# Every second column block of an up projection by seven block products, in a fused decoder layer

## The chip, the cores and the metric

The kernel runs on one core of a Trainium2 chip. The metric is the device time of one execution in microseconds (us); lower is better. All data is float32. The engines are named as in the profile: PE is TensorE's matmul, PEld its weight load, DVE is VectorE, ACT is ScalarE, POOL is GpSimd, SP is SyncE, which here only issues DMA transfers.

## The reference

One decoder layer over 512 positions and 1024 channels: a mixer (mLSTM heads and a gated long convolution), and then a feed-forward part with a causal convolution over 3 positions. The change lies in the feed-forward part:

```python
D_MODEL = 1024; SEQ = 512
D_FF = 2816                                  # 22 column blocks of 128
...
u = rms_norm(x, ffn_pre_g[l]) * (1.0 + sc2) + sh2
up = causal_dwconv(u @ ffn_up[l], ffn_conv_w[l], ffn_conv_b[l])   # (512,1024) @ (1024,5632)
a, gt = jnp.split(up, 2, axis=-1)
f = (jax.nn.silu(gt) * a) @ ffn_down[l]                           # (512,2816) @ (2816,1024)
x = x + g2 * rms_norm(f, ffn_post_g[l])
```

## The kernel before, in words

**Precision.** Each float32 operand of a large product is split into a high part (a rounded copy by ACT) and a low part (the rest, a subtraction by DVE or POOL). A product is then three matmuls, high by high, high by low and low by high (`mm3`, L188 to L190).

**Up projection.** It goes in 22 units, `for i in range(NF)`. Unit i takes column block i of the `a` half and column block i of the gate half: a weight tile `wup` of 128 x 2048, which is 16 blocks of 128 x 128 (8 along the 1024 channels for each half), 1 MB. `w_load` brings it in with one transfer on SP's queue into one of two `raws` buffers, and `w_split` cuts it into four quarters: ACT writes the high part (L170), POOL the low one (L171), into the 20 tiles of `wpool` (a quarter takes two). The matmuls write two PSUM banks, `pa` and `pg` (features by tokens, 128 x 512), 8 x 3 matmuls of 512 columns each, so 48 in a unit. The moving operand is the normalized activation, `u2h` and `u2l`, stored as two token halves of 256 (`th`), each with 8 channel blocks. Units 0 to 2 (`NE = 3`) are worked early, in token halves, so with matmuls of 256 columns; units 3 to 21 follow one after the other.

**What follows a unit.** `conv3` (L995 on ACT, L997 twice on DVE) reads each bank into an SBUF tile, ACT applies SiLU to the gate (L1057), and DVE multiplies into `F` (L1060). Two units fill one `F`; after each odd unit `forms(m, F)` makes group m's operands of the down projection: four sums on DVE (L1021 to L1024), two splits (L1013, L1014) into four slots `fh`, `fl`, and two transfers that send other parts out to `g2_d`. A slot is a 128 x 512 tile, and there are 44. The eleven groups' pairs need all 44 by the end.

**Down projection.** It is already done by seven block products. A first pass over the 11 groups (`prod1`: p1, p5, p7, p6, 24 matmuls of 512 columns for each group) needs `forms1(m)`: the weights of `load1(m)` (768 KB), three sums and four splits on DVE and ACT (L1099 to L1101, L1013, L1014). The p5 banks are the two `cv` banks, p1 the two `at` banks, p6 and p7 the four `mm` banks. A second pass (`prod2`) takes the remaining products with operands loaded again. Groups 0 to 10 come in order, and a bank is summed over all of them.

**Order.** SP's and PE's instructions are issued in the order of the program text. DVE, ACT and POOL are ordered by a planner that lists the work with a cost model, in the order of the text where several things are ready; a tile of a pool is given to the first instruction that writes it, once one is free. All transfers of weights are on SP's queue, so a transfer that waits for its buffer holds back those behind it. `load1(0)` and `load1(1)` go to `raws`, `load1(2)` to a tile that lies where `u2h` was.

Of the kernel before, what the change touches and what calls it, by code (L numbers as in the profile page):

```python
# [52 lines left out]
def decoder_layer(ctx, tc, w_glu0, x, xT, c, adaT, vecs, w_glu, w_qko, w_v0, w_v, w_out, w_up, w_down, out):  # L53
# [105 lines left out]
    def ada_done(a, b):  # L159
        V.tensor_tensor(out=mod[:, a:b], in0=mod[:, a:b], in1=vcols("ada_b", a, b - a), op=ALU.add)  # L160
# [3 lines left out]
    def w_split(src, name, pool=None, tag="w", eng=None):  # L164

        n = src.shape[1]
        pool = pool or wpool
        hi = pool.tile([P, T], F32R, tag=tag, name=f"{name}h")
        lo = pool.tile([P, T], F32R, tag=tag, name=f"{name}l")
        S.activation(hi[:, :n], src, AF.Copy)  # L170
        (eng or G).tensor_tensor(out=lo[:, :n], in0=src, in1=hi[:, :n].bitcast(F32), op=ALU.subtract)  # L171
        return hi, lo

    def w_load(view, name, pool=None, tag="w"):

        n = view.shape[1]
        r = raws.tile([P, 2048], F32, tag="raw", name=name)
        nc.sync.dma_start(r[:, :n], view)
        return [w_split(r[:, a : min(a + T, n)], f"{name}_{a}", pool, tag) for a in range(0, n, T)]

    def blk(pieces, b):
        hi, lo = pieces[b // 4]
        a = (b % 4) * P
        return hi[:, a : a + P], lo[:, a : a + P]

    def mm3(ps, a, b, start, stop):

        PE.matmul(ps, a[0], b[0], start=start, stop=False)  # L188
        PE.matmul(ps, a[0], b[1], start=False, stop=False)  # L189
        PE.matmul(ps, a[1], b[0], start=False, stop=stop)  # L190
# [459 lines left out]
    def send_rows(a, n, queue=nc.scalar):  # L650

        ps = mmbank(f"gT{a}") if a == KT else atbank(f"gT{a}")
        PE.transpose(ps[:n, :P], gains[:, a : a + n], ident)
        t = slot(f"gTs{a}")[:, :P]
        V.tensor_copy(t[:n, :], ps[:n, :P])
        for i in range(n // KT):
            queue.dma_start(rows_d[a // KT + i].rearrange("(j p) -> j p", p=P), t[i * KT : (i + 1) * KT, :])

    def row(i, make, name, queue=nc.scalar):

        rows = make(name) if make is not cvtile else [make(f"{name}r{hf}") for hf in range(2)]
# [327 lines left out]
    def halves(z):  # L989
        return z.rearrange("p (h t) -> p h t", h=2)  # L990
# [21 lines left out]
    def split(src, hi, lo):  # L1012
        S.activation(hi, src, AF.Copy)  # L1013
        behind_turn(V.tensor_tensor(out=lo, in0=src, in1=hi.bitcast(F32), op=ALU.subtract))  # L1014

    def forms(m, F):

        a11, a21, a12, a22 = (F[:, b * HT : (b + 1) * HT] for b in range(4))
        s1, s2 = ysum[:, :HT], ysum[:, HT:]
        s4 = ysq[:, (m % 2) * HT : (m % 2 + 1) * HT]  # L1020
        V.tensor_tensor(out=s1, in0=a21, in1=a22, op=ALU.add)  # L1021
        V.tensor_tensor(out=a21, in0=a11, in1=a21, op=ALU.subtract)
        V.tensor_tensor(out=s2, in0=s1, in1=a11, op=ALU.subtract)
        V.tensor_tensor(out=s4, in0=a12, in1=s2, op=ALU.subtract)  # L1024
        own = []
        for n, z in enumerate((F[:, :T], ysum)):
            hi, lo = slot(f"fh{m}_{n}", F32R), slot(f"fl{m}_{n}", F32R)
            split(z, hi, lo)
            own.append((hi, lo))
        pairs.append(own)  # L1030
        nc.scalar.dma_start(g2_d[m][:, :T], F[:, T : 2 * T])
        nc.scalar.dma_start(g2_d[m][:, T:], s4)

    for i in range(NF):
        if i < NE:
            pa, pg = early[i]
        else:
            pieces = w_load(w_up[i], f"wup{i}")
            if i in (4, 8, 12, 16):
                ada_block(38 + i // 2, last_lo[0])  # L1040
                ada_block(39 + i // 2, last_lo[0])
            if i == 19:
                ada_done(40, 48)
                gain(3, 40, "ffn_post_g")
                send_rows(3 * KT, KT)
                wide = adas.tile([P, D], F32, tag="ada", name="g2r")
                g2r = row(3, lambda n: [wide[:, :T], wide[:, T:]], "g2")
            both = []
            for half in range(2):
                ps = mmbank(f"up{i}_{half}")  # L1050
                for k in range(KT):
                    mm3(halves(ps), blk(pieces, half * KT + k), (u2h[:, :, k, :], u2l[:, :, k, :]), k == 0, k == KT - 1)
                both.append(ps)
            pa, pg = both
        a = conv3(pa, i, f"fa{i}")
        g = conv3(pg, NF + i, f"fg{i}")
        S.activation(g, g, AF.Silu)  # L1057
        if i % 2 == 0:
            F = vpool.tile([P, 2 * T + 8], F32, tag="vh", name=f"F{i // 2}")
        V.tensor_tensor(out=F[:, (i % 2) * T : (i % 2 + 1) * T], in0=a, in1=g, op=ALU.mult)  # L1060
        if i % 2:
            forms(i // 2, F)


    M1 = NM - 2
# [12 lines left out]
    def parts(r, names):  # L1078
# [3 lines left out]
            split(r[:, b * T : (b + 1) * T], hi, lo)  # L1082
            out[name[:2]] = (hi, lo)
        return out

    def quarter(r, b):
        return r[:, b * T : (b + 1) * T]

    loaded = {}

# [247 lines left out]
```

## Time and profile before

| | us |
|---|---|
| median of 3 timed runs | 773.92 (772.5 to 774.72) |
| span of the profiled execution, first to last instruction | 771.4 |
| median less span: what lies around the instructions | 2.5 |
| PE busy | 758.4 (98%) |
| DVE busy | 610.1 (79%) |
| ACT busy | 403.8 (52%) |
| POOL busy | 352.2 (46%) |
| granted TensorE clock, mean | 0.997 |

The profiled execution has no timed run of its own, so the span and the runs are set against each other as in the third row. Within the span, units 3 to 21 of the up projection run from 453.1 to 660.0, the down projection from 660.0 to about 755. In rows of the timeline the columns are start, duration, engine, line, operation, output and inputs, and in brackets the idle time before it with what ended it. Rows of windows give the busy time of each engine within a stretch and the count of instructions. Rows of groups give busy time and the mean in ns.

### The profile page before, as it was taken

What the parts mean: (1) busy time and instruction counts of PE and PEld (TensorE: products, weight loads), DVE (VectorE), ACT (ScalarE), POOL (GpSimd) and SP (SyncE); (2) the same over time, 40 slices, a digit from 0 to 9 for tenths busy, and PEclk for the clock granted to TensorE, in tenths of its full rate; (3) what the DMA queues carried; (4) which work ended last, traced back from release to release, by engine and by line L of the source; (5) the groups of instructions that cost most, each with busy time, mean ns of one, the idle gap of its engine ahead of it and who ended that gap; (6) DMA issues with size and microseconds to landing.
All of it is one profiled execution on the core that took longest, in us unless ns stands there. A gap on an engine that the chain in (4) does not pass through costs nothing.

```text
span 771.4 us, 10631 instructions
## 1 busy us (share of the span) xinstructions
PE 758.4 (98%) x3709; PEld 637.5 (83%) x3709; DVE 610.1 (79%) x967; ACT 403.8 (52%) x761; POOL 352.2 (46%) x286
## 2 busy tenths in 40 slices
PE   7999999999999999999999999999999999999996
PEld 5788898778888888988888998888888888888885
DVE  6997999999999966756768798666556687799995
ACT  5447266776666447582253555444444444455762
POOL 2029578696798645443661456444444440000001
PEclk9999999999999999999999999999999999999998
DMA  8983214214022452434953753332233321777872
GB/s 320 377 301 132 90 55 164 82 40 151 30 84 107 153 179 105 164 110 164 366 199 126 253 197 130 130 130 88 110 117 129 130 89 62 255 271 241 298 260 109
DMA packets 36409, 125.33 MB, mean 162 GB/s; under 512 B 4194, under 2 KB 5634, under 8 KB 30468
## 3 DMA queue, kind: packets, MB, share of 16 engines
q1 hardware_dynamic: 24372, 96.17, 35.5%
q10 hardware_dynamic: 11984, 28.48, 10.6%
q8 instruction: 29, 0.48, 0.3%
q14 instruction: 24, 0.20, 0.1%
HBM read 113.22 MB, written 11.42 MB: 162 GB/s over the span
## 4 chain that ended last, share of the span: by engine, by line
PE 72%; DVE 21%; DMA 2%; ACT 2%; issue 2%; POOL 0%; ACTq 0%; DVEq 0%; POOLq 0%
PE up L189 10%; PE up L188 10%; DVE cv L731 10%; PE up L190 10%; PE p L1185 4%; PE glu L189 3%; PE glu L190 3%; PE glu L188 3%; PE p L189 3%; PE p L188 3%; PE p L190 3%; PE mixa L188 2%; PE mixa L190 2%; PE mixa L189 2%; PE mixb L189 2%; PE mixb L188 2%
## 5 line engine op out<-in xcount | busy, mean ns | idle before, releaser
L731 DVE SCALAR_TENSOR_TENSOR cv<-gt,cvw,cv 128x505 f32<-128x505 f32 (+24 forms) x200 | 137.3, 729 | 2.3 <-ACT cv L719 1.1
L685 POOL TENSOR_TENSOR ro2r<-ro2t,mhalf 128x1 f32<-128x1 f32 x1 | 0.5, 537 | 119.8 <-DVE ro2t L683 119.8
L727 POOL TENSOR_TENSOR cs<-cs,cs 128x510 f32<-128x510 f32 (+3 forms) x32 | 41.9, 1308 | 0.3
L171 POOL TENSOR_TENSOR wup_1024l<-wup,wup_1024h 128x512 fp32r<-128x512 f32 x20 | 27.4, 1372 | 31.6 <-ACT wup_1024h L170 31.6
L171 POOL TENSOR_TENSOR wup_0l<-wup,wup_0h 128x512 fp32r<-128x512 f32 x20 | 27.7, 1387 | 30.0 <-ACT wup_0h L170 30.0
L171 POOL TENSOR_TENSOR wup_1536l<-wup,wup_1536h 128x512 fp32r<-128x512 f32 x20 | 28.0, 1399 | 27.6 <-ACT wup_1536h L170 25.1
L155 DVE SCALAR_TENSOR_TENSOR junk<-ada,cb 128x1024 bf16<-128x1024 f32 x20 | 31.3, 1565 | 8.5 <-DMA ada<-in_adaT 8.4
L189 PE MATMUL up<-u2l,wup_0h 128*128 128x512 f32 (+1 forms) x100 | 36.5, 365 | 0.2 <-DVE u2l L910 0.2
L188 PE MATMUL up<-u2h,wup_0h 128*128 128x512 f32 (+1 forms) x100 | 36.5, 365 | 0.0
L188 PE MATMUL up<-u2h,wup_1024h 128*128 128x512 f32 (+1 forms) x100 | 36.4, 364 | 0.0
L190 PE MATMUL up<-u2h,wup_0l 128*128 128x512 f32 (+1 forms) x100 | 36.4, 364 | 0.0
L188 PE MATMUL up<-u2h,wup_512h 128*128 128x512 f32 (+1 forms) x100 | 36.4, 364 | 0.0
L189 PE MATMUL up<-u2l,wup_512h 128*128 128x512 f32 (+1 forms) x100 | 36.4, 364 | 0.0
L190 PE MATMUL up<-u2h,wup_512l 128*128 128x512 f32 (+1 forms) x100 | 36.4, 364 | 0.0
L188 PE MATMUL up<-u2h,wup_1536h 128*128 128x512 f32 (+1 forms) x100 | 36.4, 364 | 0.0
L189 PE MATMUL up<-u2l,wup_1536h 128*128 128x512 f32 (+1 forms) x100 | 36.4, 364 | 0.0
L190 PE MATMUL up<-u2h,wup_1536l 128*128 128x512 f32 (+1 forms) x100 | 36.4, 364 | 0.0
L190 PE MATMUL up<-u2h,wup_1024l 128*128 128x512 f32 (+1 forms) x100 | 36.4, 364 | 0.0
L189 PE MATMUL up<-u2l,wup_1024h 128*128 128x512 f32 (+1 forms) x100 | 36.3, 363 | 0.0
L171 POOL TENSOR_TENSOR wup_512l<-wup,wup_512h 128x512 fp32r<-128x512 f32 x20 | 27.7, 1383 | 14.0 <-ACT wup_512h L170 14.0
L725 ACT ACTIVATE cs<-gt,cvw 128x511 f32<-128x511 f32 (+4 forms) x40 | 27.4, 716 | 6.5 <-POOL cs L727 3.2
L170 ACT ACTIVATE wup_1024h<-wup 128x512 fp32r<-128x512 f32 x22 | 13.9, 631 | 25.1 <-PE up L189 20.4
(1072 smaller groups left out, 2667.0 us busy)
## 6 DMA issues: line engine op xcount, KB each, us to landing
wup<-in_w_up SPq DMA_DIRECT2D x22, 1024.0 KB, 6.5
wqko<-in_w_qko SPq DMA_DIRECT2D x12, 1024.0 KB, 4.8
ada<-in_adaT ACTq DMA_DIRECT2D x20, 512.0 KB, 4.6
ada<-in_adaT SPq DMA_DIRECT2D x16, 512.0 KB, 6.9
wo<-in_w_out SPq DMA_DIRECT2D x8, 1024.0 KB, 4.8
spare<-in_adaT ACTq DMA_DIRECT2D x12, 512.0 KB, 7.4
wd<-in_w_down SPq DMA_DIRECT2D x6, 768.0 KB, 6.7
g2kept<-g2d SPq DMA_DIRECT2D x11, 384.0 KB, 7.3
```

Source lines behind the costliest of these rows:

```text
L155: t = V.scalar_tensor_tensor(out=junk, in0=r, scalar=1.0, in1=cb, op0=ALU.mult, op1=ALU.mult, accum_out=mod[:, i : i + 1])
L170: S.activation(hi[:, :n], src, AF.Copy)
L171: (eng or G).tensor_tensor(out=lo[:, :n], in0=src, in1=hi[:, :n].bitcast(F32), op=ALU.subtract)
L188: PE.matmul(ps, a[0], b[0], start=start, stop=False)
L189: PE.matmul(ps, a[0], b[1], start=False, stop=False)
L190: PE.matmul(ps, a[1], b[0], start=False, stop=stop)
L685: G.tensor_tensor(out=r, in0=t, in1=mhalf[:, :1], op=ALU.pow)
L725: S.activation(t[:, d:], cvx[j][:, : T - d], AF.Copy, scale=w(CK - 1 - d))
L727: G.tensor_tensor(out=side[:, d:], in0=side[:, d:], in1=t[:, d:], op=ALU.add)
L731: last_tap[0] = V.scalar_tensor_tensor(out=cp[:, d:], in0=cvx[j][:, : T - d], scalar=w(CK - 1 - d), in1=cp[:, d:], op0=ALU.mult, op1=ALU.add)
L1185: PE.matmul(ps[q], x, y, start=False, stop=m == NM - 1 and i == 2, skip_group_check=True)
```

## The change

Units 8, 10, ... 20 are computed as a 2 x 2 block product with seven products in place of eight. The weight tile's quarters are A11, A12 (`a` half, channels 0 to 511 and 512 to 1023), A21, A22 (gate half); the activation's are B11, B21 (token half 0) and B12, B22 (token half 1). A product has 4 channel blocks x 3 matmuls of 256 columns. `first_products` does four of them, then the following odd unit is done whole as before (`plain_unit`), and `last_products_up` does the other three, adding to banks in which DVE has put the sums of the first four.

- The sums of activations (`tforms`, t1 to t4) are made once, in two halves behind units 4 and 6, by POOL (high and low added), DVE (sums) and ACT and DVE (splits). They stay in 16 of the 44 slots.
- The sums of weights are made by DVE in the raw tile (`first_forms`, `last_forms`); seven splits on ACT and POOL.
- From unit 9 on, the odd units' low parts come from `added_split`: ACT writes the high part and its negative, and a transfer issued by POOL adds the raw weights to the negative. The odd units use the two `cv` banks, the seven-product units two `mm` banks and one `at` bank.
- As the slots don't suffice, the pairs of groups 0 to 3 are sent to memory on ACT's queue (16 transfers of 256 KB) and loaded again on SP's queue after the last unit's weights and ahead of the first down weights. The down projection takes the groups in the order 4 to 10, 0 to 3.
- The work for the last gain row moves from unit 19 to unit 18 (`asides`).

```diff
+    SUNITS = tuple(range(8, NF, 2))
+    SPILLED = 4
+    ORDER = [*range(SPILLED, NM), *range(SPILLED)]
+    own_d = [dram.tile([P, 4 * T], F32, tag=f"own{m}", name=f"own{m}") for m in range(SPILLED)]
+    B11, B21, B12, B22 = ([(u2h[:, th, kh * NT + k, :], u2l[:, th, kh * NT + k, :]) for k in range(NT)] for th, kh in ((0, 0), (0, 1), (1, 0), (1, 1)))
+    tforms = {n: [] for n in ("t1", "t2", "t3", "t4")}
...
+    def token_forms(j):
+        full = {}
+        for n, th, kh in (("b12", 1, 0), ("b11", 0, 0), ("b22", 1, 1), ("b21", 0, 1)):
+            ks = slice(kh * NT + 2 * j, kh * NT + 2 * j + 2)
+            full[n] = slot(f"{n}_{j}")
+            G.tensor_tensor(out=full[n], in0=flat(u2h[:, th, ks, :]).bitcast(F32), in1=flat(u2l[:, th, ks, :]).bitcast(F32), op=ALU.add)
+        b11, b12, b21, b22 = (full[n] for n in ("b11", "b12", "b21", "b22"))
+        V.tensor_tensor(out=b22, in0=b22, in1=b12, op=ALU.subtract)
+        V.tensor_tensor(out=b12, in0=b12, in1=b11, op=ALU.subtract)
+        V.tensor_tensor(out=b11, in0=b22, in1=b11, op=ALU.add)
+        V.tensor_tensor(out=b21, in0=b21, in1=b11, op=ALU.subtract)
+        for n, z in (("t1", b12), ("t3", b22), ("t2", b11), ("t4", b21)):
+            hi, lo = slot(f"{n}h{j}", F32R), slot(f"{n}l{j}", F32R)
+            split(z, hi, lo)
+            tforms[n] += [tuple(y[:, h * HT : (h + 1) * HT] for y in (hi, lo)) for h in range(2)]
...
+    def added_split(r, i, q):
+        hi, lo = (wpool.tile([P, T], F32R, tag="w", name=f"wup{i}_{q}{n}") for n in "hl")
+        S.activation(hi, quarter(r, q), AF.Copy)
+        S.activation(lo, quarter(r, q), AF.Copy, scale=-1.0)
+        G.dma_start(lo, quarter(r, q), accum_op=ALU.add)
+        return hi, lo
+    def form_product(ps, w, b, start, stop):
+        for k in range(NT):
+            a = tuple(z[:, k * P : (k + 1) * P] for z in w)
+            for n, (x, y) in enumerate(((a[0], b[k][0]), (a[0], b[k][1]), (a[1], b[k][0]))):
+                PE.matmul(ps, x, y, start=start and k == 0 and n == 0, stop=stop and k == NT - 1 and n == 2, skip_group_check=True)
+    def first_forms(i):
+        r = up_load(i)
+        a11, a21, a22 = quarter(r, 0), quarter(r, 2), quarter(r, 3)
+        w = [w_split(a11, f"wup{i}_p1")]
+        V.tensor_tensor(out=a11, in0=a11, in1=a21, op=ALU.subtract)
+        V.tensor_tensor(out=a21, in0=a21, in1=a22, op=ALU.add)
+        w.append(w_split(a21, f"wup{i}_p5"))
+        w.append(w_split(a11, f"wup{i}_p7"))
+        V.tensor_tensor(out=a11, in0=a22, in1=a11, op=ALU.subtract)
+        w.append(w_split(a11, f"wup{i}_p6"))
+        return r, w
+    def first_products(i, w):
+        X, Z, W = mmbank(f"upx{i}"), mmbank(f"upz{i}"), atbank(f"upw{i}")
+        p15, u2 = slot(f"p15_{i}"), slot(f"u2_{i}")[:, :HT]
+        form_product(X[:, :HT], w[0], B11, True, False)
+        form_product(X[:, HT:], w[1], tforms["t1"], False, True)
+        S.activation(p15[:, HT:], X[:, HT:], AF.Copy)
+        form_product(Z[:, :HT], w[2], tforms["t3"], True, False)
+        form_product(W[:, :HT], w[3], tforms["t2"], True, True)
+        S.activation(p15[:, :HT], W[:, :HT], AF.Copy)
+        V.tensor_tensor(out=u2, in0=X[:, :HT], in1=p15[:, :HT], op=ALU.add)
+        V.tensor_tensor(out=Z[:, :HT], in0=Z[:, :HT], in1=u2, op=ALU.add)
+        V.tensor_tensor(out=Z[:, HT:], in0=Z[:, :HT], in1=p15[:, HT:], op=ALU.add)
+        V.tensor_tensor(out=X[:, HT:], in0=X[:, HT:], in1=u2, op=ALU.add)
+        return X, Z
+    def last_forms(i, r):
+        a11, a12, a22 = quarter(r, 0), quarter(r, 1), quarter(r, 3)
+        V.tensor_tensor(out=a11, in0=a12, in1=a11, op=ALU.subtract)
+        return [w_split(z, f"wup{i}_{n}") for n, z in (("p2", a12), ("p3", a11), ("p4", a22))]
+    def last_products_up(banks, w):
+        X, Z = banks
+        form_product(X[:, :HT], w[0], B21, False, True)
+        form_product(X[:, HT:], w[1], B22, False, True)
+        form_product(Z[:, :HT], w[2], tforms["t4"], False, True)
+    def plain_unit(i):
+        if i < NE:
+            return early[i]
+        if i < SUNITS[0]:
+            pieces = w_load(w_up[i], f"wup{i}")
+            bank = mmbank
         else:
-            pieces = w_load(w_up[i], f"wup{i}")
...
+            r = up_load(i)
+            pieces = [added_split(r, i, q) for q in range(4)]
+            bank = cvbank
...
-    for i in range(NF):
...
+    for m in range(NM):
+        F = vpool.tile([P, 2 * T + 8], F32, tag="vh", name=f"F{m}")
+        i = 2 * m
+        asides(i)
+        if i in SUNITS:
+            r, w = first_forms(i)
+            banks = first_products(i, w)
+            unit_out(i + 1, plain_unit(i + 1), F)
+            last_products_up(banks, last_forms(i, r))
+            unit_out(i, banks, F)
+        else:
+            for i in (2 * m, 2 * m + 1):
+                unit_out(i, plain_unit(i), F)
+                if i in (4, 6):
+                    token_forms(i // 2 - 2)
+        forms(m, F)
+        if m < SPILLED:
+            for n, pair in enumerate(pairs[m]):
+                for e, z in enumerate(pair):
+                    nc.scalar.dma_start(own_d[m][:, (2 * n + e) * T : (2 * n + e + 1) * T], z.bitcast(F32))
+    g2r = g2[0]
+    for m in range(SPILLED):
+        pairs[m] = [(slot(f"fh{m}_{n}b", F32R), slot(f"fl{m}_{n}b", F32R)) for n in range(2)]
+        for n, pair in enumerate(pairs[m]):
+            for e, z in enumerate(pair):
+                nc.sync.dma_start(z.bitcast(F32), own_d[m][:, (2 * n + e) * T : (2 * n + e + 1) * T])
+    pairs = [pairs[m] for m in ORDER]
+    g2_d = [g2_d[m] for m in ORDER]
+    w_down = [w_down[m] for m in ORDER]
```

`up_load` is the load of `w_load` alone, `quarter(r, b)` is columns 512 b to 512 b + 511 of the raw tile, `flat` joins the last two dimensions, and `unit_out` is the convolution, SiLU and product that stood in the loop.

More of the change, by code (lines that the diff above doesn't have):

```diff
@@ L1032, in forms, with flat @@
         nc.scalar.dma_start(g2_d[m][:, T:], s4)
-    for i in range(NF):
+    SUNITS = tuple(range(8, NF, 2))
[4 more added lines that the diff above has]
+    tforms = {n: [] for n in ("t1", "t2", "t3", "t4")}
+    def flat(z):
+        return z.rearrange("p k t -> p (k t)")
@@ new lines, in up_load, with quarter @@
+    def up_load(i):
+        r = raws.tile([P, 2048], F32, tag="raw", name=f"wup{i}")
+        nc.sync.dma_start(r, w_up[i])
+        return r
+    def quarter(r, b):
+        return r[:, b * T : (b + 1) * T]
+    def added_split(r, i, q):
[4 more added lines that the diff above has]
+        return hi, lo
@@ L1035, in decoder_layer @@
+    def plain_unit(i):
         if i < NE:
-            pa, pg = early[i]
-        else:
-            pieces = w_load(w_up[i], f"wup{i}")
[L1039 to L1054, printed above, removed]
+            return early[i]
+        if i < SUNITS[0]:
+            pieces = w_load(w_up[i], f"wup{i}")
+            bank = mmbank
+        else:
+            r = up_load(i)
+            pieces = [added_split(r, i, q) for q in range(4)]
+            bank = cvbank
+        both = []
+        for half in range(2):
+            ps = bank(f"up{i}_{half}")
+            for k in range(KT):
+                mm3(halves(ps), blk(pieces, half * KT + k), (u2h[:, :, k, :], u2l[:, :, k, :]), k == 0, k == KT - 1)
+            both.append(ps)
+        return both
@@ L1055, in decoder_layer, with unit_out @@
+    def unit_out(i, banks, F):
+        pa, pg = banks
         a = conv3(pa, i, f"fa{i}")
@@ L1057, in decoder_layer, with asides @@
         S.activation(g, g, AF.Silu)
-        if i % 2 == 0:
-            F = vpool.tile([P, 2 * T + 8], F32, tag="vh", name=f"F{i // 2}")
         V.tensor_tensor(out=F[:, (i % 2) * T : (i % 2 + 1) * T], in0=a, in1=g, op=ALU.mult)
-        if i % 2:
-            forms(i // 2, F)
+    def asides(i):
+        if i in (4, 8, 12, 16):
+            ada_block(38 + i // 2, last_lo[0])
+            ada_block(39 + i // 2, last_lo[0])
+        if i == 18:
+            ada_done(40, 48)
+            gain(3, 40, "ffn_post_g")
+            send_rows(3 * KT, KT)
+            wide = adas.tile([P, D], F32, tag="ada", name="g2r")
+            g2.append(row(3, lambda n: [wide[:, :T], wide[:, T:]], "g2"))
+    g2 = []
+    for m in range(NM):
[27 more added lines that the diff above has]
+    w_down = [w_down[m] for m in ORDER]
     M1 = NM - 2
@@ L1084, in parts @@
         return out
-    def quarter(r, b):
-        return r[:, b * T : (b + 1) * T]
     loaded = {}
```

## The prediction

> **What bounds the kernel now.** I read the busy shares first, then the chain that ended last, then the up stage: its matmuls in order of time and every engine's load per pair of column blocks.
>
> ```profile
> span 771.4 us, 10631 instructions
> PE 758.4 (98%) x3709; PEld 637.5 (83%) x3709; DVE 610.1 (79%) x967; ACT 403.8 (52%) x761; POOL 352.2 (46%) x286
> PE 72%; DVE 21%; DMA 2%; ACT 2%; issue 2%; POOL 0%; ACTq 0%; DVEq 0%; POOLq 0%
> ```
>
> TensorE (PE) is busy 98% of the span. But busy time counts overlapping matmuls, so the distance between starts is what an edit can shorten. Two forms stand in the up stage: 512 columns, which the change removes, and 256 columns, which the early blocks 0 to 2 use and the seven products will use.
>
> ```profile
> 656.61 0.39 PE L188 MATMUL up<-u2h,wup_1024h 128*128 128x512 f32 x1
> 659.78 0.39 PE L190 MATMUL up<-u2h,wup_1536l 128*128 128x512 f32 x1
> 660.01 0.39 PE L188 MATMUL p<-b_0h,fh 128*128 128x512 f32 x1
> 434.39 0.28 PE L188 MATMUL up<-u2h,wup_1536h 128*128 128x256 f32 x1
> 445.91 0.28 PE L188 MATMUL up<-u2h,wup_1536h 128*128 128x256 f32 x1
> ```
>
> From 656.61 to 660.01 lie 15 steps, 0.2267 us each; the first down product follows the last up product with no gap. From 434.39 to 445.91 lie 96 steps (two whole blocks' halves) of 0.1200 us. So half the columns cost 0.53 of the time, and a new weight tile per matmul does not show at 256 columns.
>
> The other engines, for pairs of blocks (the first row is one block; 507.3 and 638.0 start a pair):
>
> ```profile
> core 0: us, PE busy (x) PEld busy (x) DVE busy (x) ACT busy (x) POOL busy (x), PEclk, DMA share, GB/s
> 496.40:507.30 10.90, 10.90 (x49) 9.01 (x48) 5.25 (x6) 4.38 (x7) 5.52 (x5) 1.00 0.36 131
> 507.30:529.10 21.80, 21.80 (x98) 18.05 (x97) 13.35 (x16) 9.81 (x16) 10.36 (x8) 1.00 0.33 116
> 638.00:660.00 22.00, 22.00 (x98) 18.21 (x97) 15.73 (x26) 9.31 (x15) 0.00 (x0) 1.00 0.12 45
> 660.00:670.00 10.00, 10.00 (x46) 8.27 (x45) 7.15 (x13) 4.68 (x9) 0.00 (x0) 1.00 0.87 306
> 670.00:680.00 10.00, 10.00 (x46) 8.29 (x45) 10.00 (x19) 6.78 (x14) 0.00 (x0) 1.00 0.94 340
> 760.00:771.40 11.40, 4.89 (x22) 3.73 (x20) 6.38 (x11) 2.75 (x8) 1.08 (x2) 0.82 0.37 138
> ```
>
> In the up stage PE alone is full. A microsecond saved there counts, as long as weights and sums come in time. In the down stage VectorE (DVE) is nearly full too, so work pushed across the changeover at 660 finds little room.
>
> **The change part by part.** The profile's span is 771.4 and the median of the runs 773.92; the 2.5 us around the span are taken as unchanged, and every term is added to 773.92.
>
> *PE, removed.* Units 8, 10, ... 20 (seven) take 84 matmuls of 256 columns instead of 48 of 512: 48 x 0.2267 = 10.88 against 84 x 0.1200 = 10.08, so -0.80 each, -5.6 us in all. A pair then lasts 5.76 (four products), 10.88 (the plain odd unit), 4.32 (three products) = 20.96 us.
>
> The Trainium skill's "TensorE: Matmul & The Clock Gate" (section "Back-to-back issue gap") gives 518 cycles at 512 columns and 262 at 256. By these the saving would be 48 x 0.2158 - 84 x 0.1092 = 1.19 per unit, 8.3 in all; the trace's steps are longer, and the sum keeps them.
>
> *DVE in a pair.* Its pieces:
>
> ```profile
> L1014 DVE TENSOR_TENSOR fl<-ysum,fh 128x512 fp32r<-128x512 f32 x1 | 1.6, 1632 | 0.0
> L1060 DVE TENSOR_TENSOR F<-fa8c,fg8c 128x512 f32<-128x512 f32 x1 | 1.4, 1367 | 1.0 <-ACT fg8c L1057 1.0
> L1014 DVE TENSOR_TENSOR fl<-F,fh 128x512 fp32r<-128x512 f32 x1 | 0.7, 674 | 0.0
> L1021 DVE TENSOR_TENSOR ysum<-F 128x256 f32<-128x256 f32 x1 | 0.4, 424 | 0.0
> L171 POOL TENSOR_TENSOR wup_1024l<-wup,wup_1024h 128x512 fp32r<-128x512 f32 x2 | 2.6, 1296 | 2.9 <-ACT wup_1024h L170 2.9
> L170 ACT ACTIVATE wup_1024h<-wup 128x512 fp32r<-128x512 f32 x2 | 1.3, 632 | 2.8 <-PE up L189 2.8
> L995 ACT ACTIVATE fg8c<-up,vec 128x512 f32<-128x512 f32 x1 | 0.8, 764 | 0.0
> ```
>
> The same subtraction takes 0.67 or 1.63 us; I read the long ones as running beside GpSimd (POOL). Added are four sums of weights, 128x512 (0.67 to 1.63), and four bank sums, 128x256 (0.42, the nearest row): +4.4 to +8.2 on 13.35, that is 17.8 to 21.6 in 20.96. The upper end needs every sum to collide, but POOL now subtracts 7 times 1.30 = 9.1 per pair, not 10.4, so the middle, 19 to 20, is likelier. It fits with 1 to 2 us to spare: cost 0. If that cover is gone, 0.6 us a pair, 4 in all. *ACT:* seven splits of 0.63, eight copies of 0.63 for the odd unit, two half copies (at most 0.63 each), with the convolution's four (0.76) and four more: about 17 in 20.96, hidden.
>
> *POOL.* Eight subtractions become seven plus four accumulating transfers. No row shows a transfer issued by POOL. The nearest are SP's issues (0.33, quoted below) and the subtraction that each replaces (1.30); I take 1.0, nearer the latter, since that is a row of POOL itself: 9.1 + 4 = 13 of 20.96, hidden. Each transfer waits at POOL for ACT's negated copy, and the even unit's subtractions queue behind it. The weight pool's 20 tiles are ten split pairs of the eleven in a period, so a split leads its matmul by some 18 us; 256 KB loads land in 5 to 7 us (issue table). That covers it.
>
> *Start-up at units 4 and 6.* DVE gets 16 operations for the sums of activations, POOL 8, ACT 8. DVE: 16 x 0.67 = 10.9, or some 15 beside POOL, against 5.65 idle in the one block quoted (496.4 to 507.3). Over the four blocks before unit 8 idle time is of that size; the last form (t4) is due 16 us after unit 8 starts. I take 0, bounded by 0 and 4. Spills: 16 issues on ACT's queue, 16 x 0.33 = 5.3 us over units 1 to 7, where ACT is busy 4.38 of 10.9: hidden.
>
> *The changeover, the costly step.* SP's queue is in program order, and the 16 reloads stand between unit 21's weights and the first down weights. Before:
>
> ```profile
> 624.13 12.13 SPq L1093 DMA_DIRECT2D wd<-in_w_down  x2
> 635.93 0.33 SPq L1093 DMA_DIRECT2D wd<-in_w_down  x1
> 636.22 0.69 DVE L1014 TENSOR_TENSOR b_0l<-wd,b_0h 128x512 fp32r<-128x512 f32 x1
> 640.22 0.69 DVE L1099 TENSOR_TENSOR wd<-wd 128x512 f32<-128x512 f32 x1 [3.31 <-DMA wd<-in_w_down]
> 660.21 0.33 SPq L1093 DMA_DIRECT2D wdmore<-in_w_down  x1
> wup<-in_w_up SPq DMA_DIRECT2D x22, 1024.0 KB, 6.5
> x<-in_x ACTq DMA_DIRECT2D x8, 256.0 KB, 7.0
> xr<-x1d SPq DMA_DIRECT2D x8, 256.0 KB, 6.1
> g2d<-F ACTq DMA_DIRECT2D x11, 256.0 KB, 2.0
> ```
>
> Two groups of down weights were issued 36 and 24 us before 660, and the first two groups (2 x 7 operations, 7 x 0.68 = 4.8 each) were largely split before PE came to them. The second load took 640.22 - 635.93 = 4.3. After, let 0 be unit 20's start, so the up stage ends at 20.96. A reload needs a free slot of 44: groups 4 to 9 hold 24, the activation forms 16, unit 20's partial sums 2. Twelve are freed as the first four products end (to 5.76), two when DVE has summed the banks (about 8.5), the last four only at 20.96, which group 10 can take. So the last reload goes out at about 9, the first down load at 9.7, behind about 0.5 MB (1.6 us at the 340 GB/s of 670 to 680): it lands at 9.7 + 1.6 + 4.3 = 15.6, 14 if parts overlap. That is before 20.96, so PE need not wait for data. But from 15 on DVE owes 4.8 per group, and units 21 and 20 owe 4 convolution steps and a product each (4 x 0.74 + 0.68 = 3.7 apiece) and group 10's forms 3.0. A down group takes PE 24 x 0.2267 = 5.44. By the third group (31.8) DVE owes 2 x 4.8 + 7.4 + 1.3 = 18.3 without group 10's forms, 21.3 with them, and has 16.8: late by 1.5 to 4.5. PE, never idle here before, cannot get this back. I take +2.6, nearer the low end as group 10 is used seventh now and can wait; bounds 0 (reloads out by 5) and 8 (first load 4 us later, all of DVE's list ahead).
>
> Sum: 773.92 - 5.6 + 2.6 = 770.9 us.
>
> **The rivals.**
> - *A, the forecast:* 770.9, own range 769.5 to 771.5.
> - *B, the changeover is hidden:* DVE puts group 10's forms behind the down weights, and reloads find slots early. For it: 44 - 24 - 16 = 4 are free ahead of time. Then 773.9 - 5.6 = 768.3.
> - *C, the changeover eats the gain:* the first load lands 3 us later still, as SP waits for DVE's bank sums in a full DVE queue. PE then stands still 5.6 us: 773.9. In one piece it could slow the clock: in the last row of windows, where PE is busy 4.89 of 11.4 us, the granted clock is 0.82. At 0.82 the next 5 us of matmuls take 1.1 longer: 775.0. Against it: DVE's idle 5 to 6 us per pair are there to sum the banks in.
>   The same page of the Trainium skill (Part 1, on the clock gate) says that an idle window of about 3.4 us halves the clock; by that one window at half clock would cost 1.7 us. The tail's 0.82 agrees in direction, and the trace shows no such gap inside the kernel.
> - *D, the other side: POOL becomes the bound of a pair.* Place: its in-order queue in pairs 4 to 10. If an issue holds it c us with its wait, a pair needs 9.1 + 4c; above 20.96, so from c = 2.97, POOL sets the pair. At c = 3.5 the excess is 2.1 x 7 = 15: 770.9 + 15 = 786; at 3.2, 0.94 x 7 = 6.6: 777.5. For it: a landed transfer took 2.0 to 7.0 us above, so an issue that waits for the one before would reach this. Against: issues on SP and ACT don't wait so.
> - *E, the products don't shorten:* the step at 256 columns would have to be 10.88/84 = 0.1295 or more. The 96 steps at 0.1200 speak against it. Then 773.9 + 2.6 = 776.5.
>
> **How the numbers follow.** Chances: A 0.36, B 0.12, C 0.27, D 0.21 (with the DVE overload and the start-up, which cost 4 each on the same pairs), E 0.04. A measurement of this kernel tells about 0.3%, 2.3 us. A and B are faster: 0.48. C lies mostly within: 0.25, and 0.02 of it is slower. D and E are slower: 0.25, so slower 0.27. Range 768.0 (B, with a little less lost around it) to 780.0, which holds B, A, C, E and D up to c = 3.3.
>
> **What would show it.** Steps of 0.120 in the products of units 8 to 20; a pair in 21.0 us; POOL 13 and DVE 18 to 20 of it; the first load of down weights issued about 11 us before the last up matmul; PE waits of 2 to 3 us in all, on DVE's splits, within the first three down groups. Wrong if a pair takes over 21.3, if POOL's queue shows long waits on ACT or a transfer, or if PE waits at the changeover by more than 5 us or not at all.

## The result, and the profile after

The change makes the kernel slower: 820.79 us in the median (819.09 to 823.45, four executions) against 773.21 for the kernel before beside it (771.77 to 774.72); ratio 1.0621, 95% interval 1.0594 to 1.0648. The page of the profile after, with the sum of its chain by engine:

```profile
span 819.4 us, 11429 instructions
PE 766.4 (94%) x3961; PEld 655.5 (80%) x3961; DVE 648.2 (79%) x1039; ACT 435.9 (53%) x832; POOL 380.9 (46%) x315
PE 56%; DVE 22%; DMA 10%; issue 5%; ACT 4%; POOL 2%; SPq 0%; ACTq 0%; DVEq 0%; POOLq 0%
```

No other engine became full: the busy shares of DVE, ACT and POOL are those of before within a point. PE went from 98% to 94%, and DMA from 2% to 10% of the chain. So the loss is waiting. Four rows of PE's timeline after show where (start, duration, engine, line, operation, output and inputs, idle time before with its releaser):

```profile
506.56 0.28 PE L1082 MATMUL upx<-u2h,wup_p1h 128*128 128x256 f32 x1
508.60 0.28 PE L1082 MATMUL upx<-t1h,wup_p5l 128*128 128x256 f32 x1
...
683.48 0.28 PE L1082 MATMUL upz<-t4h,wup_p4l 128*128 128x256 f32 x1
704.69 0.80 PE L188 MATMUL p<-b_0h,fh 128*128 128x512 f32 x1 [20.94 <-ACT b_0h L1013]
```

From 506.56 to 508.60 lie 17 steps of 0.120 us, so a product's price is the forecast one. The seven pairs last from 506.56 to 683.60, 177.0 us; before, 14 units took 14 x 10.88 = 152.3, and the forecast was 7 x 20.96 = 146.7. Then PE stands still for 21 us. Against the forecast span (771.4 - 3.0 = 768.4) the 51.0 us that it is off are made up so:

| stretch | forecast | measured | difference |
|---|---|---|---|
| start of unit 8 | 507.7 | 506.6 | -1.1 |
| seven pairs | 146.7 | 177.0 | +30.3 |
| from the last up matmul to the first down matmul | 2.6 (with the waits after it) | 21.1 | +18.5 |
| down projection to the end | 111.4 | 114.7 | +3.3 |

PE's waits from 506 to 710 (total, times, longest):

```profile
PE p L188 <- ACT b_0h L1013: 20.9, 1, 20.9
PE upx L1082 <- DVE upx L1109: 9.3, 3, 4.0
PE upx L1082 <- ACT wup_p5h L170: 6.7, 2, 3.7
PE upx L1082 <- ACT t1h L1013: 1.8, 1, 1.8
PE upx L1082 <- DVE t1l L1014: 1.5, 1, 1.5
```

In the pairs that is 19.3 us: 3.3 in unit 8, for the first activation sums (t1), and 16.0 in the five pairs of units 10 to 18, each time between the plain unit and the last three products. The other 11 us of the 30.3 are mostly slower steps. Unit 8's pair lasted 27.3 us (506.56 to 533.84), 6.3 over the forecast; the six others together are 24.0 over. Two windows of after in the pairs, as long as a pair of before, and two around the changeover (busy time of PE, PEld, DVE, ACT and POOL, then the granted clock, DMA share, GB/s):

```profile
507.30:529.10 21.80, 18.53 (x91) 16.32 (x90) 19.22 (x29) 13.12 (x25) 9.65 (x10) 0.84 0.71 211
...
594.40:616.20 21.80, 17.81 (x103) 16.33 (x102) 13.46 (x23) 13.54 (x25) 10.67 (x11) 0.84 0.50 143
...
680.00:700.00 20.00, 3.75 (x32) 3.55 (x30) 8.57 (x14) 4.12 (x7) 0.00 (x0) 0.72 0.44 139
700.00:720.00 20.00, 15.30 (x57) 12.04 (x58) 15.42 (x26) 8.23 (x16) 0.00 (x0) 0.76 0.86 314
```

From 594.40 DVE, ACT and POOL have 8 to 11 of 21.8 us to spare, and PE still waits. The clock falls with the waits: 0.84, where it was 1.00.

**The cycle of the raw buffers.** A pair needs two loads of weights, and there are two `raws` buffers. The load of the next even unit waits for the buffer that the odd unit's transfers read. One turn of this cycle in the timeline after, from the load of unit 16 to that of unit 18, while PE is at units 15 and 14:

```profile
593.23 1.83 SPq L1064 DMA_DIRECT2D wup<-in_w_up  x2
...
599.07 0.63 ACT L170 ACTIVATE wup_p1h<-wup 128x512 fp32r<-128x512 f32 x1 [4.00 <-DMA wup<-in_w_up]
...
600.65 0.36 ACT L1102 ACTIVATE p<-upx 128x256 f32<-128x256 f32 x1
...
605.24 0.55 PE L1082 MATMUL upx<-u2h,wup_p2h 128*128 128x256 f32 x1 [3.99 <-DVE upx L1109]
...
608.53 1.29 POOL L171 TENSOR_TENSOR wup_p6l<-wup,wup_p6h 128x512 fp32r<-128x512 f32 x1 [1.47 <-ACT wup_p6h L170]
609.90 0.88 POOL L1075 DMA_DIRECT2D wup_0l<-wup  x1
...
613.55 0.87 POOL L1075 DMA_DIRECT2D wup_3l<-wup  x1 [0.69 <-PE upx L1082]
...
619.50 0.81 SPq L1064 DMA_DIRECT2D wup<-in_w_up  x2
```

5.8 us to land, 10.8 until the four split pairs of the even unit are through ACT, DVE and POOL, 3.7 to issue the odd unit's four transfers behind them, and 6.0 until the last has landed and SP may load again: 26.3 us, where PE needs 20.96. It is the longest of five turns: the loads of units 10, 12, ... 20 leave at 516.95, 542.32, 567.89, 593.23, 619.50 and 644.88, 25.6 us apart in the mean, and units 10 to 20 start 25.8 us apart (533.84 to 662.62). The waits of SP's queue and of ACT say the same:

```profile
SPq L1064 <- DMA wup_3l<-wup: 128.1, 6, 29.9
...
ACT wup_p1h L170 <- DMA wup<-in_w_up: 26.0, 6, 7.0
```

The transfers, from the issues (count, KB each, median us to landing):

```profile
wup_0l<-wup POOLq DMA_DIRECT2D x7, 256.0 KB, 3.4
...
wup_3l<-wup POOLq DMA_DIRECT2D x7, 256.0 KB, 5.1
```

Each turn ACT stands 4 us at `wup_p1h`, which is the *next* even unit's first split. Behind it in ACT's queue are the copies of p5 and p6 (L1102, L1105) of the unit *in work*. DVE's sums need those, and PE's last three products need the sums. That is how a late load of the next unit stops PE in this one.

**The changeover.** SP's queue after:

```profile
667.26 0.78 SPq L1185 DMA_DIRECT2D fl_1b<-own  x1
673.70 0.32 SPq L1185 DMA_DIRECT2D fh_0b<-own  x1
677.15 0.32 SPq L1185 DMA_DIRECT2D fl_0b<-own  x1
685.87 0.32 SPq L1185 DMA_DIRECT2D fh_1b<-own  x1
691.19 0.32 SPq L1185 DMA_DIRECT2D fl_1b<-own  x1
...
695.74 0.99 SPq L1216 DMA_DIRECT2D wd<-in_w_down  x2
```

Its waits at the reloads:

```profile
SPq L1185 <- DMA g2d<-ysq: 15.0, 3, 6.9
SPq L1185 <- DMA g2d<-F: 13.9, 2, 8.3
```

Four reloads leave by 667.26, as unit 20's first products run (the unit starts at 662.62). The next four wait 21.9 us in all, for transfers of the last groups' parts to land: the seventh leaves at 685.87 and the eighth at 691.19. So the first down weights leave at 695.74, 12 us after the last up matmul and not 11 before it, as forecast, and the first split of them starts at 704.01.

### The profile page after: what moved, and what is told of

It is laid out like the page before. It is cut to its first block, busy times and chain, and to the rows that moved or that the text cites. A ratio compares the mean times of both kernels' runs of the same rounds, so it can differ in the third digit from the quotient of the medians.

```text
span 819.4 us, 11429 instructions
## 1 busy us (share of the span) xinstructions
PE 766.4 (94%) x3961; PEld 655.5 (80%) x3961; DVE 648.2 (79%) x1039; ACT 435.9 (53%) x832; POOL 380.9 (46%) x315
## 4 chain that ended last, share of the span: by engine, by line
PE 56%; DVE 22%; DMA 10%; issue 5%; ACT 4%; POOL 2%; SPq 0%; ACTq 0%; DVEq 0%; POOLq 0%
DVE cv L731 10%; PE up L189 5%; PE up L188 4%; PE up L190 4%; PE p L1308 4%; DMA wup<-in_w_up 3%; PE glu L189 3%; PE glu L190 3%; DMA wup_3l<-wup 3%; PE glu L188 3%; PE p L188 3%; PE p L189 3%; PE p L190 3%; PE upx L1082 2%; PE mixa L188 2%
## 5 line engine op out<-in xcount | busy, mean ns | idle before, releaser
L155 DVE SCALAR_TENSOR_TENSOR junk<-ada,cb 128x1024 bf16<-128x1024 f32 x20 | 30.3, 1516 | 8.5 <-DMA ada<-in_adaT 8.2
L1014 DVE TENSOR_TENSOR fl<-F,fh 128x512 fp32r<-128x512 f32 x11 | 11.8, 1073 | 18.2 <-ACT fh L1013 18.2
L188 PE MATMUL up<-u2h,wup_0h 128*128 128x512 f32 (+1 forms) x72 | 25.6, 356 | 0.0
L190 PE MATMUL up<-u2h,wup_0l 128*128 128x512 f32 (+1 forms) x72 | 25.4, 353 | 0.0
L171 POOL TENSOR_TENSOR wqko_1024l<-wqko,wqko_1024h 128x512 fp32r<-128x512 f32 x12 | 16.3, 1359 | 18.4 <-ACT wqko_1024h L170 12.9
L155 DVE SCALAR_TENSOR_TENSOR junk<-spare,cb 128x1024 bf16<-128x1024 f32 x12 | 19.0, 1586 | 3.4 <-DMA spare<-in_adaT 3.2
L188 PE MATMUL p<-b_0h,fh 128*128 128x512 f32 x2 | 1.4, 714 | 20.9 <-ACT b_0h L1013 20.9
L188 PE MATMUL qko<-uh,wqko_1024h 128*128 128x512 f32 x48 | 20.6, 430 | 0.0
L188 PE MATMUL qko<-uh,wqko_0h 128*128 128x512 f32 x48 | 20.2, 420 | 0.0
L276 DVE SCALAR_TENSOR_TENSOR junk<-ada,cb 128x1024 bf16<-128x1024 f32 x16 | 19.5, 1218 | 0.1
L171 POOL TENSOR_TENSOR wo_512l<-wo,wo_512h 128x512 fp32r<-128x512 f32 x8 | 12.9, 1615 | 13.7 <-ACT wo_512h L170 13.7
L171 POOL TENSOR_TENSOR wqko_0l<-wqko,wqko_0h 128x512 fp32r<-128x512 f32 x12 | 16.6, 1384 | 4.9 <-ACT wqko_0h L170 4.8
```

The costliest lines, as they stand in the source:

```text
L276: V.scalar_tensor_tensor(out=junk, in0=first[k][:, i * D : (i + 1) * D], scalar=1.0, in1=cb, op0=ALU.mult, op1=ALU.mult, accum_out=part[k] ...
```

## The experiments

The buffer theory says: the pairs are paced by the two raw buffers, and the accumulating transfers are what makes their cycle long. Its rival, the order theory: no cycle, but the splits of the next unit stand ahead of the copies in ACT's queue. For the changeover, the queue theory: SP's program order costs the 21 us, and nothing else does. The rival there: DVE's backlog takes its place. The kernel before took 771.49 to 772.12 beside these runs. Where no interval is given, the time is one execution's; four executions of one kernel (spaced_order) lay up to 4.7 us apart, so smaller differences between such runs are read from the waits in the traces.

**The reloads later** (reload_late). Each group's four reloads are issued behind a down step's own loads, in steps 0 to 3.

```diff
-    for m in range(SPILLED):
-        pairs[m] = [(slot(f"fh{m}_{n}b", F32R), slot(f"fl{m}_{n}b", F32R)) for n in range(2)]
...
         if m < 5:
             load_g2(m)
+        if m < SPILLED:
+            reload(m)
```

> The sixteen reloads of the spilled pairs no longer stand on SP's queue ahead of the first down weights; each group's four follow the down weights of one of the first four down groups. Queue theory: the 21 us in which PE stands still at the changeover, and the 2 to 3 us at a low clock behind it, are the wait of the first down load behind the reloads; the load then goes out during the last pair as before the change, PE waits under 3 us at the changeover, and the time falls by 19 to 23 us, to 798 to 802. Rival, the work of VectorE pushed across the changeover: 4 to 8 us of waiting stay: 803 to 808. Rival, the reloads now hold up the later down weights: PE waits inside the first pass instead, and the gain is under 10 us. The pairs of units 8 to 21 are untouched by this and stay at 25 us.

Measured: 810.74, span 808.8. PE's waits:

```profile
PE upx L1082 <- DVE upx L1109: 17.4, 4, 9.4
```

The 21 us are gone, but one wait of 9.4 is new, in the last pair: the down weights now come early, and ACT and DVE work on them ahead of unit 20's copies and sums (its copies on ACT start at 676.76, behind four splits of down weights from 671.70 on). The queue theory is half right: 10.1 us are saved of the 19 to 23 expected. The other half goes to the order on the other engines.

**Subtraction in place of the transfers** (odd_subtract).

```diff
-            pieces = [added_split(r, i, q) for q in range(4)]
+            pieces = [w_split(quarter(r, q), f"wup{i}_{q}") for q in range(4)]
```

> The odd units' low parts come from subtractions on GpSimd as before the change, in place of a negated copy and an accumulating transfer; nothing else is changed. Buffer theory: a pair of units takes 25.3 us since the two raw weight buffers go round in a cycle: load 6, the four forms one after the other 11, then the transfers, which stand behind them on GpSimd's queue, 3.6 to issue and 5 to land, and only then the next load. Without the landing and the copies a cycle is 3 to 4 us shorter, 21.5 to 22.5: seven pairs save 20 to 26 us, so 795 to 801. Rival, throughput of GpSimd and VectorE: GpSimd has 11 subtractions of 1.3 us, 14.3 in a pair in place of 9.1 + 3.5, and VectorE's sums collide more: a pair stays at 25 or gets longer, 818 to 828. Rival, the order on ScalarE: as far as the next load comes earlier, the wait of the copies behind it goes too, so this run can't tell that from the buffer theory; the next one can.

Measured: 801.77, span 799.9, just past the 795 to 801 of the buffer theory and far from its rival's 818 to 828. Windows (the rows between are alike):

```profile
557.50:578.80 21.30, 21.22 (x135) 19.02 (x134) 17.34 (x24) 11.59 (x23) 15.30 (x12) 1.00 0.32 118
...
621.60:643.00 21.40, 21.23 (x134) 19.03 (x133) 17.64 (x25) 10.76 (x21) 14.44 (x12) 1.00 0.38 142
```

One turn of the raw buffer in the timeline:

```profile
585.11 4.54 SPq L1064 DMA_DIRECT2D wup<-in_w_up  x2
...
604.73 1.75 POOL L171 TENSOR_TENSOR wup_3l<-wup,wup_3h 128x512 fp32r<-128x512 f32 x1
...
606.51 4.54 SPq L1064 DMA_DIRECT2D wup<-in_w_up  x2
```

POOL is busier (14.4 to 15.3 a pair, not 9.3 to 12.1), and the pairs are faster: 21.3 to 21.4 us at a full clock. The load leaves as the odd unit's last subtraction ends (604.73 + 1.75), 21.40 us after the one before, and PE's pair is as long. The buffer theory holds, and the buffers still set the pace, by 0.4 us.

**The order on ACT** (act_order). The next unit's first split is queued behind the copies of the unit in work, with the transfers left in.

```diff
         w = [w_split(a11, f"wup{i}_p1")]
+        if last_p15:
...
+            tc.add_manual_dep(ins, last_p15[-1].ins.name, mybir.DependencyInfo(mybir.DependencyClass.NoSync, mybir.DependencyReason.DATA),
+                              reason="order on ScalarE")
...
+        last_p15.append(S.activation(p15[:, :HT], W[:, :HT], AF.Copy))
```

> One order edge on ScalarE: the first split of the next seven-product unit is queued behind the copies of the partial sums of the unit before; nothing else is changed. Order theory: PE waits at the second half of the products since those copies stand in ScalarE's queue behind a split that waits for its weights; with the edge the five gaps of 3 to 4 us at that place go and with them the low clock, a pair takes 21 to 22 us, and the time falls by 20 to 28 us, to 793 to 801. Buffer theory: the gaps go from that place, but PE then waits ahead of the first products for the weights, as their cycle still takes 24 to 25 us; the time falls by under 8 us.

Measured: 821.04, no gain. PE's waits:

```profile
PE p L188 <- ACT b_0h L1013: 20.6, 1, 20.6
PE up L190 <- DMA wup_0l<-wup: 13.1, 6, 5.2
```

The wait moved to the first quarter of the plain unit. Unit 20 starts 8.4 us earlier than in after (654.19 for 662.62), but its weights' load leaves only 0.8 us earlier (644.05 for 644.88), and the last pair gives the lead back, 5.2 us of it in one wait for a transfer. The order theory falls as the cause: order only chose at which matmul the late buffer is met.

**The three together** (three_parts).

> All three edits together: reloads behind the down weights, odd units' low parts by subtraction on GpSimd, and the order edge on ScalarE. If the losses are those three and independent: the pairs at 21 to 22 us and a changeover under 3 us, so 770 to 778. By the throughput rival a pair stays above 24 us: 795 or more.

Measured: 790.68, span 788.7, more than expected. Left are the start (3.1 and 0.8 us of waits for t1, and 0.84 of the clock), 0.3 to 1.0 us in each pair from 10 to 18, and 4.0 in unit 20 behind down work. The down stage takes 117.5 us (788.7 - 671.2), 6.1 more than before; PE's waits there for DVE's convolutions are 1.7, and the rest is not explained.

**The start, apart** (start_10). Subtraction, and the first unit by seven products is 10:

```diff
-    SUNITS = tuple(range(8, NF, 2))
+    SUNITS = tuple(range(10, NF, 2))
```

> As odd_subtract (801.8), but the first unit by seven products is 10 in place of 8, so the sums of activations have two plain units more. Start-up theory: in unit 8 PE waits 4.8 us for t1 and then runs at half clock, 7 to 8 us in all; these go, and one unit's saving of 0.8 goes with them: 794 to 796. Rival: the sums of activations are late because the planner lays them between other work of VectorE, wherever they are due; PE then waits as long in unit 10: 801 to 803.

Measured: 799.39. The waits for the activation sums are gone and the clock there is 1.00, but the five waits at the last products are 7.2 us in all (2.5 in odd_subtract), so the gain is 2.4 of the 6 to 8 expected. A turn of the raw buffers takes 22.3 to 23.2 us here (loads at 533.09, 555.38, 577.92, 600.38 and 623.62), and not 21.4; the runs don't show why it is longer.

**The changeover, apart** (changeover_alone). The kernel after with the reloads spread, two tiles in each of down steps 0 to 7, and the first down sums and splits queued behind unit 20's bank sums and copies.

```diff
+        if m < 2 * SPILLED:
+            reload(m // 2, m % 2)
...
+        queued(V.tensor_tensor(out=t3, in0=b22, in1=b12, op=ALU.subtract), sums[1])
```

> The changed kernel with the changeover alone taken back: the reloads spread, two tiles behind each of the first eight steps of the down projection, and the first down weights' split and sums queued behind unit 20's copies and bank sums; the transfers of the odd units stay. Queue theory: in reload_late the gain was halved because ScalarE and VectorE took up the first down weights, which were still on their way, ahead of unit 20's copies, a new wait of 9.4 us; with the edges that goes, and the full 20.9 of waiting and the low clock behind it are saved: 797 to 801. Rival, VectorE's work pushed over: PE then waits for the down splits instead: 803 to 809.

Measured: 802.14, 18.7 us less, between the two ranges expected and near the queue theory's. The 20.9 us wait shrinks to 2.2 and 0.9 us on DVE's convolutions of unit 20 (fa20c, fg20c). These are the waits that the forecast had for the whole changeover.

**Subtraction and the mended changeover, from unit 10, with and without the order at the changeover** (both_10, both_10_no_edge).

> Subtraction on GpSimd, first unit 10, reloads spread and the order edges at the changeover, together. Six units save 0.8 each, 4.8, against the kernel before, and a pair measured 21.3 in odd_subtract, 0.35 above the sum of its steps, so 2.1 of it is lost. If nothing is lost at the changeover: 769. With 2 to 4 us of waiting for VectorE there: 771 to 773. If the parts hide further losses: above 776.

> As both_10 without the order edges. If the new wait of reload_late came of the order in which ScalarE and VectorE take the first down weights, it comes back: 4 to 10 us above both_10. If it came of the transfers alone (their buffer being late), the two are equal.

Measured: 782.37 with it, 786.83 without, 4.5 us apart. Without it the wait in unit 20 is back (5.8 us, and none there with it) and the first down matmul comes 9.5 us later (671.5 for 662.0); the down stage is then 5.0 us shorter. So the order matters, and half of what it saves is lost behind it. Both are above 776, so losses were still hidden. ACT's timeline with the order shows the one in the pairs:

```profile
560.49 0.64 ACT L170 ACTIVATE wup_p1h<-wup 128x512 fp32r<-128x512 f32 x1 [5.22 <-DMA wup<-in_w_up]
561.03 0.62 ACT L1158 ACTIVATE fg10c<-fg10c 128x512 f32<-128x512 f32 x1
564.47 0.64 ACT L1015 ACTIVATE fh<-F 128x512 fp32r<-128x512 f32 x1 [2.82 <-DVE F L1027]
...
566.11 0.39 ACT L1114 ACTIVATE p<-upx 128x256 f32<-128x256 f32 x1
```

It is the picture of after once more: 5.2 us at the next unit's split, and the SiLU, the splits of F and the copies all behind it.

**The order on ACT, with the buffers' cycle shortened** (both_10_order).

> The kernel of both_10 (odd units by subtraction, first seven-product unit 10, reloads two tiles a step, changeover in order), with the first weight split of the next unit queued on ScalarE behind the copies of the unit before. Order theory: the five gaps of 1.3 to 2.2 us (9.1 us) at the last three products go with it: span 780.6 - 9.1 = 771.5, time 773. Buffer theory (the two raw buffers set the pace, a split held back only hands a buffer on later): the gaps turn up at the plain unit's first weights, time 780 to 785.

Measured: 778.29 (ratio 1.0073, interval 1.0056 to 1.0089). Windows of two pairs and of the first down steps:

```profile
549.80:570.80 21.00, 21.00 (x134) 19.11 (x133) 17.25 (x24) 10.89 (x21) 15.07 (x11) 1.00 0.33 120
...
612.80:634.90 22.10, 21.32 (x135) 19.09 (x134) 17.43 (x25) 12.51 (x22) 14.76 (x11) 1.00 0.37 130
...
660.00:680.00 20.00, 14.74 (x55) 11.89 (x55) 20.00 (x36) 9.71 (x17) 0.00 (x0) 0.83 0.80 294
```

Units 12, 14, 16 and 18 start at 549.84, 570.82, 591.80 and 612.86: pairs of 20.98, 20.98 and 21.06 us with no wait in them. Of the five waits in units 10 to 18 only that in 18 is left (0.8), and unit 20 has one (1.6). So order counts after all, once the buffers nearly keep up; with the transfers it saved nothing. The buffers still don't quite keep up: the loads of units 12, 14, 16 and 18 leave at 534.19, 556.67, 578.58 and 600.47, 21.9 us or more apart, so they lead their units' starts by 15.7, 14.2, 13.2 and 12.4 us. The waits in units 18 and 20 follow on that; that the shrinking lead causes them is argued, not tested. The up stage now ends at 657.8 (660.0 before). What it saved is spent at once: DVE is 20.00 of 20 busy from 660 on, PE waits 5.3 us for fg21c, and the clock falls to 0.83. The 773 expected is missed by this.

**Fewer units by seven products**, 10, 14 and 18, with and without the order on ACT (spaced_order, spaced).

> As both_10_order, with units 10, 14 and 18 alone by seven products, the rest plain, so that two plain pairs' loads and splits lie between them. Buffer theory: the raw buffers catch up between two such units and the gaps at their last products are under 0.7 us: three units give -2.4 us, the first down steps cost what they cost in both_10 (gaps of 2.65 and 1.2 us and some 2 us of slower steps): time 772 to 776. If a seven-product unit has its gap by itself, whatever its neighbours do, three gaps of 1.8 us stay: 778 to 781.

> As spaced_order without the order on ScalarE. Buffer theory: within 1 us of spaced_order, since no load is late and the split does not wait. Order theory: gaps of 1.3 to 2.2 us stay at the three units' last products, 4 to 6 us above spaced_order.

Measured: 781.54 (1.0127, interval 1.0099 to 1.0154) and 778.79. Both theories miss. Two plain units in a row share the two `cv` banks here, and the second waits for the first's convolutions (2.1 us on fa20c, and 1.9 at unit 12's start on ACT's `wup_p6h`). So this kernel has a wait of its own, and does not tell the theories apart. The wait at the last products of unit 10 stays (1.6 to 2.3 us), but units 14 and 18 have none there.

**Units 10 to 18, the last pair plain** and in two sorts of banks (ten_to_18).

```diff
-    SUNITS = tuple(range(10, NF, 2))
+    SUNITS = tuple(range(10, 19, 2))
...
-            bank = cvbank
+            bank = cvbank if i % 2 else mmbank
```

> both_10_order with units 10, 12, 14, 16 and 18 by seven products and the last pair plain (its first unit in the other pair of PSUM banks), so that the last work of the up projection is a plain unit's. Theory: pairs of 20.98 us, and the wait of 5.26 us at the first down products (VectorE behind unit 20's and 21's convolutions) falls to the 0.5 us of spaced. Span: 771.4 - 5 x 0.80 + 1.2 for one late gap + 2.4 for the first down steps beside the reloads = 771.0, time 772 to 774, which is no change against before. If the wait belongs to the reloads and not to unit 20's last products, it stays: 776 to 778.

Measured: 775.02 (1.0031, interval 1.0019 to 1.0043), span 773.0, between the two ranges expected. It is the best of these kernels and still 0.3% slower than before. The up stage ends at 656.6, 3.4 us earlier; the down stage takes 773.0 - 656.6 = 116.4, 5.0 us longer. Windows at the changeover, and the row after the longer wait:

```profile
640.00:660.00 20.00, 18.11 (x80) 14.64 (x79) 19.93 (x35) 10.82 (x18) 0.00 (x0) 1.00 0.25 82
660.00:680.00 20.00, 19.00 (x76) 15.29 (x77) 19.14 (x34) 9.01 (x16) 0.00 (x0) 0.91 0.94 326
...
660.50 0.47 PE L188 MATMUL p<-t_0h,fh 128*128 128x512 f32 x1 [2.39 <-DVE fa21c L997]
```

DVE is nearly full for 40 us. Before, the same first window had 15.73. PE's waits for it are 2.4 and 0.5 us, and the slow steps after them cost about 0.09 x 20 = 1.8: together 4.7 of the 5.0.

A third raw buffer, the plain test of the cycle, wasn't tried.

## Why the prediction was wrong

- *PE, removed (-0.80 a unit):* right in size. Steps of 0.120 in after, and pairs of 20.98 against 20.96 in both_10_order. In the changed kernel the pairs never ran at that pace.
- *DVE, ACT, POOL at cost 0:* right that none is full (12.1 to 14.7, 9.8 to 13.5 and 9.3 to 12.1 of 21.8 from unit 10 on). DVE's range of 17.8 to 21.6 was too high, and so was ACT's 17; in both_10_order DVE has 16.6 to 17.3 in pairs 12 to 16.
- *POOL's issues taken at 1.0:* measured 0.86 to 0.89 in the pairs. Rival D as it stood, a queue full from c = 2.97 on, did not happen.
- *"so a split leads its matmul by some 18 us ... That covers it":* the step that failed, worth 24.0 us in units 10 to 21; with subtractions in place of the transfers (odd_subtract) the same six pairs are 3.6 over. It took the lead from the 20 tiles of the weight pool. The lead is set by the two raw buffers, whose cycle was not added up: load 5.8, splits 10.8, issues 3.7, landing 6.0. A transfer costs POOL 0.87 us, but from the first issue to the last landing the four held the raw buffer for 9.6 us, behind the even unit's splits. The forecast priced the engine and not the buffer. The landing of 5 to 7 us, which it read from rows of 2.0, 6.1 and 7.0, came out at 3.4 to 5.1 (medians). D looked at the right place and counted the wrong resource; its time of 786 came from 3.5 us per issue.
- *What the clock adds:* forecast at 1.1 to 1.7 us for one long wait. Waits of 1.5 to 4 us in six pairs, five of them followed by half the clock, brought about 11 us of slower steps.
- *Start-up, 0 taken, bounds 0 and 4:* the waits were 3.3, within the bounds, but the clock stayed at half for some 6 us behind them, 6.3 in all. The forecast timed t4, which is due last; PE waited for t1, due 12 x 0.12 = 1.4 us into unit 8.
- *The changeover, +2.6, bounds 0 and 8:* 21.1. "Twelve are freed as the first four products end": four reloads went as they ended, but the fifth to the eighth waited for transfers of group parts to land, and the first down load left 23 us later than forecast. What became of the other eight of the twelve slots the runs don't show. Of the sum, what the forecast had as its content, DVE's backlog, is seen in changeover_alone (2.2 and 0.9 us) and in ten_to_18 (2.4 and 0.5). Rival C had the direction, and with its wait of 5.6 us a quarter of the size, but gave DVE's bank sums as what SP waits for.
- The three conditions under "wrong if" came true: pairs over 21.3, a wait of over 5 us at the changeover, and long waits of POOL on ACT (24.0 us in all at `wup_p5l`, seven waits, up to 3.7), though POOL was never full.

Whether the change can win at all stays open. Cleared of all that was found, with five units, it saves 3.4 us up to the changeover and loses 5.0 behind it (one profile each), nearly all in waits for DVE and the slow steps after them. What makes DVE's list longer there was not taken apart, and no run here takes the spills away.

## What to carry to other kernels

Before moving work to a queue that looks idle, add up one full turn of each buffer that it reads: load, every reader in order, landing, next load. If the turn is longer than the pair of units that it serves (here 25.6 us against 20.96), the busy shares don't show it, and the wait turns up at whatever stands behind the late split in its engine's queue. And a transfer that waits for a slot in the middle of the queue that loads the next stage can cost that stage all of its lead (here 23 us).

## What was not expected of the hardware

An accumulating transfer of 256 KB within the chip's SBUF, four in a row, took POOL 0.86 to 0.89 us to issue and 3.4 to 5.1 us (medians of the first and the last) to land.

The clock's answer to a wait is not a matter of its length alone. In the kernel after, PE waited 2.93 us before 553.60, and the granted clock stayed at 1.00; it waited 2.40 us before 631.14, and got half of it for the next 3 us. Rows and windows of after:

```profile
553.60 0.36 PE L1082 MATMUL upx<-u2h,wup_p2h 128*128 128x256 f32 x1 [2.93 <-ACT wup_p5h L170]
631.14 0.55 PE L1082 MATMUL upx<-u2h,wup_p2h 128*128 128x256 f32 x1 [2.40 <-DVE upx L1109]
...
553.00:555.00 2.00, 1.40 (x12) 1.43 (x13) 1.06 (x4) 1.69 (x3) 1.42 (x2) 1.00 0.02 4
...
631.00:634.00 3.00, 2.86 (x13) 2.89 (x14) 2.28 (x4) 1.26 (x3) 1.53 (x2) 0.50 0.00 0
```

And of ten_to_18, behind its waits of 2.4 and 0.5 us:

```profile
662.00:664.00 2.00, 2.00 (x5) 1.60 (x6) 1.45 (x3) 1.03 (x2) 0.00 (x0) 0.52 0.97 376
```

In the trace's record of the clock after, the stretches at half clock in the pairs begin at 511.46, 579.72, 603.62, 630.92 and 658.23, each 7, 8 or 20 times 3.413 us after the one before. Counted in steps of 3.413 us on this grid, the wait of 2.93 us falls 1.75 and 1.18 into two of them, and of the wait of 2.40 us 2.2 lie in one.

This agrees with the Trainium skill, "TensorE: Matmul & The Clock Gate" (Part 1), which has the gate watch a free-running window of 3413 ns. The same page of the Trainium skill gives one idle window, about 3.4 us, as what throttles; the waits that were enough here, 2.40 us alone and 2.4 with 0.5 us, are shorter.
